# A planner that orders emission gets other prices: shared port, PSUM readers, table loads, products

## The chip, the cores and the metric

One core of one Trainium2 chip. The metric is the device time of one execution in microseconds, median of three runs. The core's engines run their own instruction queues in order: TensorE (PE; products, with PEld for the loading of weights), VectorE (DVE), ScalarE (ACT), GpSimd (POOL), and SyncE (SP), which issues most of the transfers.

## The reference

One inference step of a two-layer decoder trunk for 256 prompt tokens and 8 samples of 8 tokens, 320 tokens in all, width 2048, in fp32. Both groups share all weights.

```
layer 0:  h = modulate(x, c);  z = h @ ab_w_in
          GLA, 4 heads of 128 x 256, on q, k, v, r, g_lr out of z
          S5, 64 groups of 16 channels with 64 complex states, on u out of z
          y = y * sigmoid(y @ s5_w_glu + b);  x += gate * concat(o, y) @ ab_w_out
          h = modulate(x, c);  x += gate * (silu(h @ w1) * (h @ w3)) @ w2
layer 1:  h = modulate(x, c);  z = h @ ml_w_in
          mLSTM, 4 heads, matrix state 512 x 256 per head and sample
          x += gate * hh @ ml_w_out;  then a second FFN
final:    rmsnorm(x)
modulate(x, c): shift, scale, gate = silu(c) @ ada_w + ada_b, once for each of four sub-layers
```

The states of GLA, S5 and mLSTM are read, updated and written for every sample.

## The kernel before

**Products.** Every large product has the 320 tokens as its moving side. Weights come in units of 512 rows by 256 columns (`load_to`); `split_to` splits each into a rounded high part (ScalarE, `act.copy(hi, raw)`) and the rest (VectorE, `tensor_sub(lo, raw, hi)`), and `run_pair` does three products for each 128 x 128 block: high with high, low with high, high with low. Two rows of blocks and two columns make 12 products for each split of 128 x 512.

**Tasks beside the products.** After each block, `tick` may resume one or more of the Python generators that emit the recurrent layers: S5 (`s5_task`, `builder1`, `builder2`, `toep`, `gelu`, with the state scan largely on GpSimd), GLA (`gla_task` for four heads in turn, `gla_tail` for the state update of each head's eight samples), mLSTM (`ml_task`), and the modulation weights (`Ada`, whose `drip` does `run` steps every `gap` ticks; a step is four fp32 products of 32 rows, which stand in the trace as 8 records). A generator yields what it waits for: tiles, a number of ticks, or GO.

**The planner.** The order of all queues is fixed while the program is emitted, by a model of the engines. `Est` (line 130) keeps a time for each engine and, for every tile, when it is written and when it was last read. Each emitted operation goes through `note` (line 161), which adds a price to its engine's time. `tick` (line 383) resumes a task when

```
t[1] <= clock[0] and t[2] + SLACK <= est.t["PE"]
and max(est.t["DVE"], est.t["ACT"]) < est.t["PE"] + (AHEAD if t[3] >= 5 else AHS)
```

that is when its tiles are ready by the model's TensorE time and neither VectorE nor ScalarE is 2.5 us ahead. Tasks of lower rank number stand first in the list; S5's have ranks 1 to 4, GLA's 5. `mps` (line 279) picks, of three PSUM banks for small products, the one that the model sees free first. Where the main stream needs a result, `wait` (line 417) and `go` (line 404) emit a modulation step if one is ready (`spare`, line 508), else resume tasks, else emit a small warming product.

**Gates.** The output product of layer 0 runs first over S5's half of the rows, then over GLA's half, which needs the flags ("oh", h) of `conv` (line 1773), set after the last GLA head. A head's second part needs the flag of the previous head's tail, ("tail", h - 1). After mLSTM `z1_end` (line 2319) waits for the flag "nout" of the last head.

`toep` (line 1279) copies blocks out of one PSUM bank, `(act.copy if i % 2 else vec.tensor_copy)`, four by ScalarE, four by VectorE in turn. `gla_tail` does for each sample a mask on GpSimd (`km`), one product, and one VectorE addition.

Of the kernel before, what the change touches and what calls it, by code (L numbers as in the profile page):

```python
# [16 lines left out]
AF = mybir.ActivationFunctionType  # L17
# [5 lines left out]
T = 320  # L23
# [53 lines left out]
class Buf:  # L77
    def __init__(self, mem, off, n):
        self.mem, self.off, self.n = mem, off, n
# [50 lines left out]
class Est:  # L130
# [3 lines left out]
    def __init__(self):  # L134
        self.t = dict.fromkeys(("PE", "DVE", "ACT", "POOL", "SP", "DGE", "DMA"), 0.0)
        self.wr, self.rd, self.alias = {}, {}, {}
        self.end = 0.0

    def _at(self, tab, ap):
        t = ap.tensor  # L140
        name = self.alias.get(t.name, t.name)
        if ap.space == bass.MemoryType.DRAM:
            lo, hi = ap.offset, ap.offset + sum(st * (c - 1) for st, c in ap.ap)
            a = tab.setdefault(name, np.zeros(400 if len(name) < 8 else 1))
            o, n = (lo // 10240, hi // 10240 - lo // 10240 + 1) if len(a) > 1 else (0, 1)
        else:
            dims = list(ap.ap)
            row, parts = dims[0]
            a = tab.get(name)
            if a is None:  # L150
                a = tab[name] = np.zeros((4, row))
            q, o = ap.offset // row // 32, ap.offset % row
            quads = (ap.offset // row % 32 + parts + 31) // 32
            return np.lib.stride_tricks.as_strided(a[q:, o:], (quads, *(c for _, c in dims[1:])),
                                                   (8 * row, *(8 * st for st, _ in dims[1:])))
        return a[o:o + n]
# [4 lines left out]
    def note(self, eng, op, a, k):  # L161
        aps = [x for x in (*a, *k.values()) if isinstance(x, bass.AP)]
        out = k.get("out", aps[0])
        ins = [x for x in aps if x is not out and x is not k.get("accum_out")]
        n = int(np.prod(out.shape[1:]))
        t = self.t[eng]
        for x in ins:
            t = max(t, self.ready(x))
        if out.space != bass.MemoryType.DRAM:
            t = max(t, float(self._at(self.rd, out).max()))  # L170
            if eng != "PE" and op != "dma_start":
                t = max(t, self.ready(out))
        if op == "dma_start":
            if eng == "POOL":
                t = self.t[eng] = t + 1.2
            else:
                self.t[eng] = t + 0.06
                t = self.t["DGE"] = max(self.t["DGE"], t) + 0.45
            t = self.t["DMA"] = max(self.t["DMA"], t + 0.65) + 4e-3 * int(np.prod(out.shape)) / 360
            fin = t + 1.0  # L180
        else:
            if eng == "PE":
                if op == "transpose":
                    d = 0.107
                elif ins[0].shape[1] == 32:
                    d = 0.01 + 4.1e-4 * n
                elif ins[0].dtype == F32R:
                    d = n / 2400 + 0.003
                else:
                    d = max(1.67e-3 * n + 0.05, 0.2 + 5e-4 * n)  # L190
            elif eng == "ACT":
                d = 0.095 + 0.83e-3 * n
            elif eng == "POOL":
                d = 0.095 + n * (0.83e-3 if op == "memset" else 4e-3 if op == "tensor_scalar" else 2.27e-3)
            else:
                n = max(n, int(np.prod(ins[0].shape[1:]))) if op == "tensor_reduce" else n
                d = 0.065 + (6.26e-3 if op == "reciprocal" else 1.04e-3) * n
            t = self.t[eng] = t + d
            fin = t + 0.13
            self.end = max(self.end, fin)  # L200
        for x in ins:
            r = self._at(self.rd, x)
            np.maximum(r, fin, out=r)
        for x in (out, k.get("accum_out")):
            if x is not None:
                w = self._at(self.wr, x)
                np.maximum(w, fin, out=w)
# [26 lines left out]
def trunk(tc, a, o, coff, dbg=None, stop=None):  # L234
    nc = tc.nc
    est = Est()
# [3 lines left out]
    with (  # L240
# [163 lines left out]
        def go(gen):  # L404

            while True:
                est.end = 0.0
                try:
                    y = next(gen)
                except StopIteration as e:  # L410
                    return e.value
                p = est.t["PE"]
                idle(due(y)[1])
                if y is GO and est.t["PE"] == p:
                    idle(p + 0.3)
# [16 lines left out]
        class Ada:  # L432
# [75 lines left out]
            def spare(self):  # L508

                if self.s >= self.limit:  # L510
                    return False
                self.load()
                if est.ready(self.slot[self.s]) > est.t["PE"]:
                    return False
                return self.step()

# [5 lines left out]
            def drip(self):  # L522


                while self.s < 192:
                    n = min(self.run - self.s % self.run, self.last - self.s)
                    self.load()
                    if n <= 0:
                        if self.pend:
                            yield [ADAM["ev"].v(512)]  # L530
                            self.post()
                        yield self.gap
                    elif self.ld >= self.s + n and all(est.ready(self.slot[self.s + i]) <= est.t["PE"] for i in range(n)):
                        for _ in range(n):
                            self.step()
                        self.load()
                        yield self.gap
                    else:
                        yield 1
                self.post()  # L540
# [119 lines left out]
        n = 0  # L660
# [59 lines left out]
        def sums(sq):  # L720

            ps = yield from kept()
            for x, q in enumerate(sq):
                if x:
                    yield [q]
                for i, b in enumerate((0, P, 192)):
                    mm(ps[:, i:i + 1], q[:, b:b + P], ones[:, 0:1], x == 0 and i == 0, x == len(sq) - 1 and i == 2)
            yield 1
            return ps[:, 0:3]

        def rsqrt_tok(s, n):

            rs_n[0] ^= 1
            v, t, y = (rs_b.v(3, o=3 * i + 12 * rs_n[0]) for i in range(3))
            vec.tensor_scalar(v, s, 1.0 / n, EPS, MUL, ADD)
            drop(s)

            vec.tensor_scalar(y.bitcast(I32), v.bitcast(I32), 1, 0x3fffffff, ALU.logical_shift_right, ALU.bitwise_xor)
            vec.tensor_scalar(y, y, 0.957 * 2.0 ** 62.5, None, MUL)
            for _ in range(3):  # L740
                vec.scalar_tensor_tensor(t, y, -0.5, y, MUL, MUL)
                vec.tensor_mul(t, t, v)
                vec.scalar_tensor_tensor(y, t, 1.5, y, ADD, MUL)
            yield 1
            return y
# [81 lines left out]
        def resid(L, k, ps, sq):  # L827

            x, m = X[0], MOD[L]
            vec.scalar_tensor_tensor(x[:, k, 0:TP], ps[:, 0:TP], m[:, 32 + k, 0:1], x[:, k, 0:TP], MUL, ADD)  # L830
            t = gt_b.v(NB, 8, o=64 * (k % 2))
            vec.tensor_mul(t, ps[:, TP:T].rearrange("p (b t) -> p b t", b=NB),
                           m[:, 32 + k, 1:9, None].to_broadcast([P, NB, 8]))
            vec.tensor_add(x[:, k, TP:T], x[:, k, TP:T], gt_b.v(64, o=64 * (k % 2)))
            if sq:
                sq_chunk(k)
                if L == 3:
                    spawn(to_out(k), 0)
# [976 lines left out]
        for i in range(8):  # L1815
            add(Pair(a["ab_w_out"][0], 256 * i, 256, range(8, 16), act_opnd,
                     lambda j, ps, i=i: resid(0, 2 * i + j, ps, False)))
# [543 lines left out]
        n = len(first)  # L2361
# [57 lines left out]
        y = go(rsqrt_tok(go(sums([sq[:, i, :] for i in range(3)])), 2048))  # L2419
# [51 lines left out]
```

## Time and profile before

| | us |
|---|---|
| median of 3 runs | 3362.9 (3360.3 to 3363.32) |
| the profiled execution | 3362.54 |
| its span, first to last instruction | 3360.7 |
| TensorE busy | 3259.7 (97%) |
| VectorE busy | 1873.2 (56%) |
| ScalarE busy | 1328.4 (40%) |
| GpSimd busy | 332.8 (10%) |

In the trace all operations that go through the planner's wrapper carry line 220, so they are told apart by tile: `mm` are the large products, `ada` the modulation products, `misc` the small ones of the tasks, `hi` and `lo` the split weights, `S_slab` holds S5, `G_slab` and `GR_slab` hold GLA, `R_slab` mLSTM, `X_slab` the residual stream. An fp32 product stands as two records. Records of products overlap, so a product's spacing is read from a chain of many, not from its mean duration. "[7.01 <-DVE G_slab]" behind an instruction says that its engine stood idle for 7.01 us and what ended that.

### The profile page before, as it was taken

Reading aid. Unit: us, or ns where it says so; the run is one execution under the profiler, and the core shown is the slowest. Engines: PE = TensorE matmul, PEld = TensorE weight load, DVE = VectorE, ACT = ScalarE, POOL = GpSimd, SP = SyncE. Lnnn points to the kernel's source line nnn. Section 1 sums busy time; section 2 is a strip of 40 time slices with the busy share of each in tenths; the row PEclk is TensorE's granted clock in tenths of the full one; section 3 lists DMA queues with packets and bytes.
Section 4 is the critical chain, followed back from the end, with each engine's and each line's share of the span. In section 5 each row is a group of like instructions: output and inputs, shape, how many; then the busy total and the mean of one; then the engine's idle time right before and its main releaser. Section 6 shows DMA issues by size and latency. Waiting matters only on the chain.

```text
span 3360.7 us, 57787 instructions
## 1 busy us (share of the span) xinstructions
PE 3259.7 (97%) x22778; PEld 3036.6 (90%) x22778; DVE 1873.2 (56%) x3921; ACT 1328.4 (40%) x2509; POOL 332.8 (10%) x508
## 2 busy tenths in 40 slices
PE   7898899999999999999999999999999999999998
PEld 4687788998999989999998999999999999999997
DVE  3768667764444444444475665565644544545546
ACT  2364355343333333333434443344443343344343
POOL 0225411220000000000040000002200000000002
PEclk9999899999999999999999999999999999999999
DMA  9886688667767777776455664665444444444443
GB/s 304 295 266 235 205 307 301 237 235 255 258 235 273 240 255 257 236 274 201 150 165 144 194 187 140 187 188 201 145 151 151 151 151 151 150 149 150 149 150 101
DMA packets 597792, 686.66 MB, mean 204 GB/s; under 512 B 41096, under 2 KB 495056, under 8 KB 596944
## 3 DMA queue, kind: packets, MB, share of 16 engines
q1 hardware_dynamic: 594464, 680.26, 61.8%
q8 instruction: 179, 2.93, 0.3%
q10 hardware_dynamic: 3056, 2.70, 0.2%
q14 instruction: 93, 0.76, 0.1%
HBM read 643.19 MB, written 39.69 MB: 203 GB/s over the span
## 4 chain that ended last, share of the span: by engine, by line
PE 86%; DVE 5%; DMA 4%; ACT 2%; issue 1%; POOL 1%; SPq 1%; ACTq 0%; DVEq 0%; POOLq 0%
PE mm L220 73%; PE misc L220 8%; PE ada L220 4%; DVE lo L220 1%; DVE X_slab L220 1%; DVE S_slab L220 1%; POOL S_slab L220 1%; DMA fix_slab<-in_ab_ada_w_dram 1%; DVE xl L220 1%; SPq L220 1%; DMA UD<-S_slab 1%; DMA R_slab<-in_state_mlstm_C_dram 0%; DVE G_slab L220 0%; ACT hi L220 0%; DMA fix_slab<-in_ffn_ada_w_dram 0%
## 5 line engine op out<-in xcount | busy, mean ns | idle before, releaser
L220 DVE TENSOR_TENSOR lo<-fix_slab,hi 128x512 fp32r<-128x512 f32 (+1 forms) x1556 | 1089.1, 705 | 1155.2 <-ACT hi L220 1151.0
L220 PE MATMUL mm<-xh,hi 128*128 128x320 f32 x4704 | 1480.4, 315 | 10.7 <-DVE S_slab L220 7.6
L220 ACT CAST hi<-fix_slab 128x512 fp32r<-128x512 f32 (+1 forms) x1556 | 945.6, 612 | 1328.9 <-PE mm L220 1273.1
L220 PE MATMUL mm<-xh,lo 128*128 128x320 f32 x4704 | 1459.1, 310 | 1.4 <-DVE lo L220 1.4
L220 PE MATMUL mm<-xl,hi 128*128 128x320 f32 x4704 | 1459.7, 310 | 0.6 <-DVE xl L220 0.6
L220 PEld LDWEIGHTS mm<-xh,hi 128*128 128x128 f32 x4704 | 888.2, 189 | 57.5 <-issue 30.9
L220 PEld LDWEIGHTS mm<-xh,lo 128*128 128x128 f32 x4704 | 888.9, 189 | 2.8 <-DVE lo L220 2.3
L220 PEld LDWEIGHTS mm<-xl,hi 128*128 128x128 f32 x4704 | 888.1, 189 | 2.4 <-DVE xl L220 2.4
L220 PE MATMUL mm<-ffh,hi 128*128 128x320 f32 x1408 | 435.8, 310 | 0.0
L220 PE MATMUL mm<-ffh,lo 128*128 128x320 f32 x1408 | 434.3, 308 | 0.0
L220 PE MATMUL mm<-ffl,hi 128*128 128x320 f32 x1408 | 434.3, 308 | 0.0
L220 POOL TENSOR_TENSOR X_slab<-X_slab 128x320 f32<-128x320 f32 (+1 forms) x117 | 109.7, 938 | 2030.6 <-DVE X_slab L220 2015.3
L220 PEld LDWEIGHTS mm<-ffh,hi 128*128 128x128 f32 x1408 | 264.0, 188 | 6.7 <-issue 6.7
L220 PEld LDWEIGHTS mm<-ffh,lo 128*128 128x128 f32 x1408 | 264.0, 188 | 0.0
L220 PEld LDWEIGHTS mm<-ffl,hi 128*128 128x128 f32 x1408 | 264.0, 187 | 0.0
L220 PE MATMUL ada<-fix_slab 128*32 128x512 f32 x952 | 121.7, 616 | 6.4 <-DMA fix_slab<-in_ab_ada_w_dram 4.6
L220 POOL TENSOR_TENSOR S_slab<-S_slab 128x32 f32<-128x32 f32 (+3 forms) x226 | 114.1, 514 | 92.0 <-ACT S_slab L220 46.0
L220 ACT COPY fix_slab<-ada 128x512 f32<-128x512 f32 x48 | 28.1, 586 | 184.8 <-PE ada L220 184.8
L220 DVE SCALAR_TENSOR_TENSOR ffs<-ffs,mm 128x320 f32<-128x320 f32 x176 | 81.6, 488 | 22.8 <-ACT ffs L220 22.7
L220 DVE SCALAR_TENSOR_TENSOR X_slab<-mm,fix_slab,X_slab 128x256 f32<-128x256 f32 x176 | 84.6, 481 | 14.8 <-PE mm L220 14.8
L220 PEld LDWEIGHTS ada<-fix_slab 128*32 128x32 f32 x952 | 25.1, 111 | 56.7 <-issue 44.6
L220 DVE TENSOR_TENSOR S_slab<-S_slab 128x256 f32<-128x256 f32 (+3 forms) x167 | 70.6, 434 | 6.8 <-POOL S_slab L220 2.8
(153 smaller groups left out, 1923.2 us busy)
## 6 DMA issues: line engine op xcount, KB each, us to landing
fix_slab<-in_ffn_w_dram SPq DMA_DIRECT2D x524, 512.0 KB, 3.5
fix_slab<-in_ffn_ada_w_dram SPq DMA_DIRECT2D x65, 1024.0 KB, 8.7
fix_slab<-in_ml_w_in_dram SPq DMA_DIRECT2D x96, 512.0 KB, 4.7
fix_slab<-in_ab_ada_w_dram SPq DMA_DIRECT2D x35, 1024.0 KB, 7.7
fix_slab<-in_ab_w_in_dram SPq DMA_DIRECT2D x64, 512.0 KB, 7.0
adam<-in_ffn_ada_w_dram SPq DMA_DIRECT2D x31, 1024.0 KB, 8.2
adam<-in_ml_ada_w_dram SPq DMA_DIRECT2D x29, 1024.0 KB, 8.9
fix_slab<-in_ml_ada_w_dram SPq DMA_DIRECT2D x19, 1024.0 KB, 9.0
```

Source lines behind the costliest of these rows:

```text
L220: r = call(*a, **k)
```

## The change

`Est` alone is changed, and the two places that ask whether a modulation step's weights have landed. Operations, shapes and the tasks' code stay. Prices: a 320-column product in fp32r goes from n/2400 + 0.003 to n/2400 + 0.0135 us, the small fp32 products and the 32-row ones get new formulas, and changing between kinds of product costs 0.1 or 0.2. A result of TensorE is seen 0.2 instead of 0.13 us after its end. An operation that reads PSUM now starts only after the last reader of the bank on another engine. ScalarE pays 1.3 us when the function table changes (Ln, Sin, and all others that need one). The scan on VectorE costs twice as much per column. A GpSimd operation takes 15% longer when VectorE's time is ahead, and a VectorE operation with two or more inputs is lengthened by 0.9 of its overlap with the last 40 GpSimd operations. Weights of a modulation step must have been ready for 1 us.

```diff
@@ class Est, __init__
+        self.kind = self.table = None
+        self.bank = {}
+        self.pool = [(0.0, 0.0)] * 40
@@ note
         for x in ins:
             t = max(t, self.ready(x))
+            if x.space == bass.MemoryType.PSUM:
+
+                t = max([t] + [y for e, y in self.bank.get(self.alias.get(x.tensor.name, x.tensor.name), {}).items() if e != eng])
@@
                 if op == "transpose":
-                    d = 0.107
+                    kind, d = "other", 0.109
                 elif ins[0].shape[1] == 32:
-                    d = 0.01 + 4.1e-4 * n
+                    kind, d = "tiles", 4.23e-4 * n
                 elif ins[0].dtype == F32R:
-                    d = n / 2400 + 0.003
+                    kind, d = "stream" if n == T else "other", n / 2400 + 0.0135
                 else:
-                    d = max(1.67e-3 * n + 0.05, 0.2 + 5e-4 * n)
+                    kind, d = "other", max(1.667e-3 * n + 0.004, 0.222)
+
+                if kind != self.kind:
+                    d += 0.2 if "tiles" in (kind, self.kind) else 0.1
+                self.kind = kind
             elif eng == "ACT":
                 d = 0.095 + 0.83e-3 * n
+                fun = next((x for x in (*a, *k.values()) if isinstance(x, AF)), None)
+                if fun is not None and fun not in (AF.Identity, AF.Copy, AF.Square):
+                    table = fun if fun in (AF.Ln, AF.Sin) else "exp"
+                    if table != self.table:
+                        d += 1.3
+                    self.table = table
             elif eng == "POOL":
                 d = 0.095 + n * (0.83e-3 if op == "memset" else 4e-3 if op == "tensor_scalar" else 2.27e-3)
             else:
                 n = max(n, int(np.prod(ins[0].shape[1:]))) if op == "tensor_reduce" else n
-                d = 0.065 + (6.26e-3 if op == "reciprocal" else 1.04e-3) * n
+                d = 0.065 + (6.26e-3 if op == "reciprocal" else 2.1e-3 if op == "tensor_tensor_scan" else 1.04e-3) * n
+
+            if eng == "POOL" and op != "memset":
+                if self.t["DVE"] > t:
+                    d *= 1.15
+                self.pool = self.pool[1:] + [(t, t + d)]
+            elif eng == "DVE" and len(ins) > 1:
+                d += 0.9 * sum(max(0.0, min(t + d, y) - max(t, x)) for x, y in self.pool)
             t = self.t[eng] = t + d
-            fin = t + 0.13
+            fin = t + (0.2 if eng == "PE" else 0.13)
@@
         for x in ins:
+            if x.space == bass.MemoryType.PSUM:
+                self.bank.setdefault(self.alias.get(x.tensor.name, x.tensor.name), {})[eng] = fin
@@ spare
-                if est.ready(self.slot[self.s]) > est.t["PE"]:
+                if est.ready(self.slot[self.s]) + 1.0 > est.t["PE"]:
@@ drip
-                    elif self.ld >= self.s + n and all(est.ready(self.slot[self.s + i]) <= est.t["PE"] for i in range(n)):
+                    elif self.ld >= self.s + n and all(est.ready(self.slot[self.s + i]) + 1.0 <= est.t["PE"] for i in range(n)):
```

## Rows read from the trace of the kernel before

**Rows 1.** Windows: span; busy PE, PEld, DVE, ACT, POOL; clock; DMA share; GB/s
```profile
0.00:170.00 170.00, 137.23 (x849) 95.91 (x849) 93.56 (x271) 54.97 (x104) 24.44 (x44) 0.94 0.87 296
170.00:640.00 470.00, 436.74 (x3141) 376.25 (x3145) 335.25 (x893) 227.78 (x534) 139.51 (x275) 0.96 0.77 261
760.00:1680.00 920.00, 920.00 (x6452) 852.74 (x6452) 422.04 (x768) 332.82 (x569) 0.00 (x0) 1.00 0.70 240
1765.00:2275.00 510.00, 497.89 (x3697) 463.26 (x3697) 303.05 (x641) 202.81 (x395) 35.33 (x42) 0.99 0.58 174
2440.00:3270.00 830.00, 830.00 (x5661) 830.00 (x5660) 414.00 (x718) 325.36 (x554) 0.00 (x0) 1.00 0.48 150
```
**Rows 2.** Chain that ended last, dense stretch: start, us, what, how many
```profile
1600.48 142.13 PE mm L220 x969
```
**Rows 3.** Waits of PE in 170 to 640: us in total, times, longest
```profile
PE misc L220 <- ACT S_slab L220: 15.3, 6, 7.8
PE misc L220 <- DVE G_slab L220: 11.1, 6, 7.0
PE ada L220 <- DMA fix_slab<-in_ffn_ada_w_dram: 1.9, 2, 1.4
```
**Rows 4.** Timeline of PE, ACT: start, us, what, idle before and its releaser
```profile
335.44 1.97 PE L220 MATMUL misc<-S_slab 128*128 128x81 f32 x8 [7.01 <-DVE G_slab L220]
332.44 1.28 ACT L220 ACT_TABLE_LOAD   x1
393.81 0.55 PE L220 MATMUL misc<-GR_slab 96*128 96x256 f32 x1 [7.76 <-ACT S_slab L220]
392.80 0.91 ACT L220 COPY S_slab<-misc 32x128 f32<-32x128 f32 x4 [1.06 <-DVE S_slab L220]
```
**Rows 5.** Windows around the two stops, columns as in rows 1
```profile
328.00:346.00 18.00, 10.99 (x61) 10.20 (x61) 12.47 (x34) 8.39 (x23) 12.26 (x31) 0.53 0.63 219
390.00:404.00 14.00, 9.89 (x46) 7.94 (x50) 7.66 (x27) 7.13 (x22) 2.50 (x4) 0.52 0.44 124
```
**Rows 6.** Windows of the large products' tile alone: PE, PEld, DVE, ACT
```profile
170.00:640.00 470.00, 277.12 (x1716) 255.99 (x1716) 21.24 (x57) 12.47 (x28) 0.96 0.77 261
1765.00:2275.00 510.00, 367.48 (x2291) 341.19 (x2291) 0.00 (x0) 21.15 (x49) 0.99 0.58 174
```
**Rows 7.** Timeline of VectorE around 385: additions beside GpSimd, alone, and a split
```profile
380.48 5.93 DVE L220 TENSOR_TENSOR S_slab<-S_slab 128x256 f32<-128x256 f32 x8
387.53 1.80 DVE L220 TENSOR_TENSOR S_slab<-S_slab 128x256 f32<-128x256 f32 x4
389.25 0.69 DVE L220 TENSOR_TENSOR lo<-fix_slab,hi 128x512 fp32r<-128x512 f32 x1
```
**Rows 8.** GpSimd's groups in 252 to 420: count, busy us, mean ns, idle
```profile
L220 POOL TENSOR_TENSOR S_slab<-S_slab 128x32 f32<-128x32 f32 x128 | 41.3, 322 | 9.7
L220 POOL TENSOR_TENSOR S_slab<-S_slab 128x256 f32<-128x256 f32 x42 | 33.0, 805 | 42.1 <-ACT S_slab L220 41.0
```
**Rows 9.** Groups of ScalarE in 170 to 640: the table loads
```profile
L220 ACT ACT_TABLE_LOAD x9 | 11.5, 1283 | 0.1
```
**Rows 10.** Timeline of PE before the output product's second half
```profile
638.95 1.92 PE L220 MATMUL ada<-fix_slab 128*32 128x512 f32 x16
```
**Rows 11.** Timeline of PE at the end of mLSTM
```profile
2273.21 1.92 PE L220 MATMUL ada<-fix_slab 128*32 128x512 f32 x16
```
**Rows 12.** Waits of PE in 1765 to 2275, for the state blocks
```profile
PE misc L220 <- DMA R_slab<-in_state_mlstm_C_dram: 2.5, 5, 1.7
```
**Rows 13.** Timeline of PE: first and last state product of tails 0, 1
```profile
280.04 0.36 PE L220 MATMUL misc<-GR_slab 96*128 96x256 f32 x1
433.13 0.39 PE L220 MATMUL misc<-GR_slab 96*128 96x256 f32 x1
461.60 0.28 PE L220 MATMUL misc<-GR_slab 96*128 96x256 f32 x1
479.50 0.28 PE L220 MATMUL misc<-GR_slab 96*128 96x256 f32 x1
```

## The prediction, made before the change was run

> **What bounds the kernel now.** I read the busy time by stage first, because the change alters no product, no transfer and no formula; it can only alter the order in which instructions stand in the queues, and that matters only where an order is free. In the two dense stages (760 to 1680 and 2440 to 3270, together 1750 of the span's 3360.7 us) TensorE shows no idle time at all [rows 1]: products follow each other at 142.13 us for 969, 0.1467 us each [rows 2]. No task runs there except the loading of modulation products every 70 ticks, so these 1750 us stand. The first 170 us move 296 GB/s with the 16 DMA engines busy 0.87 of the time; they wait for weights, and no price of an engine changes that. What is left to an order are 170 to 640 (S5 and GLA beside the products of layer 0), 1765 to 2275 (mLSTM), and small stretches around the norms. TensorE is idle 33.3 us of the 470 in the first and 12.1 of the 510 in the second.
>
> Then I read who is waited for. In 170 to 640 two names carry it: products of S5 and GLA wait 15.3 us in 6 waits for ScalarE and 11.1 in 6 for VectorE [rows 3]. The two longest are in the timeline [rows 4]. At 328.2 TensorE stops 7.01 us for a product of S5 whose PSUM bank GLA had not yet read out: a table load of 1.28 us and a scan lie ahead of that read. At 386 it stops 7.76 us for a GLA tail product whose operand ScalarE copies only after the block copies of `toep`, where VectorE and ScalarE read one bank in turns (ScalarE waits 1.06 us for its second turn). Around each stop the granted clock is near one half: 0.53 over 328 to 346 and 0.52 over 390 to 404 [rows 5], that is the lower level, 1.2 GHz, for most of it, after TensorE had stood or done little. With 10.99 and 9.89 us of busy time there, running at 0.53 and 0.52 costs 5.2 and 4.7 us. The ceiling of the first stage is thus 33.3 + 9.9 = 43.2 us.
>
> **The change part by part.** It emits no new operation; the planner `Est` only gets other prices, and tasks are resumed at other places of the stream.
> The *product price* goes from 320/2400 + 0.003 = 0.1363 to 0.1468 us against the row's 0.1467. With 1716 products in the first free stage and 2291 in the second [rows 6] the planner's TensorE clock gains 18.0 and 24.1 us. So far a task whose data were due in L us came back after L/0.1363 products, 7.7% later in real time than needed; that cushion goes. Small fp32 products get cheaper (81 columns 0.2405 to 0.222) and each change of kind 0.1 or 0.2 us dearer; these two nearly cancel, I take nothing for them.
> The *shared port*: a VectorE addition of 128x256 takes 1.80/4 = 0.45 us alone and 5.93/8 = 0.74 beside GpSimd [rows 7]. The planner had 0.331 for both and now adds 0.9 of the overlap. GpSimd's own operations were priced 0.168 (128x32) and 0.676 (128x256); the rows of 252 to 420 have 0.322 and 0.805 [rows 8]. The new factor of at most 1.15 gives 0.193 and 0.777.
> *One reader per bank*, *table loads* (9 of 1.283 us in the stage [rows 9], priced 1.3, zero until now) and the *scan* (0.40 to 0.74) are the causes of the two long stops. I take both stops away, 14.8 us, and their slow clock, 9.9; of the other waits for ScalarE and VectorE (15.3 + 11.1 - 14.8 = 11.6) half, 5.8. That is 30 us by which TensorE gets through its products sooner; the ends are 0 and 43.
> *Ready plus 1.0* on modulation steps: it can save the 1.9 us of such waits in the stage [rows 3], and puts each step 1 us later; cover is that the steps of this stage are needed only at the norm behind the gate below, and if that cover were gone a step would cost the wait for its weights. I take nothing. The transfers that tasks issue on SP move with them; between 170 and 640 the DMA engines have 0.77 of their time taken [rows 1], so this too is nothing, with the range bearing it.
>
> **Where the 30 us go** is the question that decides. The output product of layer 0 needs the GLA heads. At 638.95 TensorE does two modulation steps as a filler (16 records, 1.92 us) [rows 10]: the planner had nothing else, because the flag of GLA was still missing. So products and GLA chain end together now. If products come 30 us sooner, TensorE stands before that gate from about 609 on, and GLA ends when it ends. Its chain is not sped up by a missing TensorE stall as such: in the 7.01 us stop VectorE and ScalarE were working for GLA. It is sped up by what is no longer beside it: each 12 products (1.76 us) cost VectorE one split of 0.69 us [rows 7], 39% of it, and VectorE is busy 335 of 470 us. For 30 us without them I take one third off the chain, 10 us (ends 0 and 30). In the other 20 us modulation steps fill in: two loaded ones and about two more, 0.96 us each by the gate's row, 4 us that later stages need not do. A slow clock after standing costs some back, 3 us. Sum: 10 + 4 - 3 = 11 us.
> The second stage ends at the same kind of gate: 16 filler records at 2273.21 [rows 11]. GpSimd hardly works there (35 of 510 us), its stops are short and partly for DMA. Without the cushion tasks come back sooner; I take 1 us of gain, the ends being -12 (all idle time) and +16 (all 32 state blocks waited for, at the 2.5/5 = 0.5 us that five of them cost now [rows 12]). The profiled execution took 3362.54, 1.84 over its span, and the median is 3362.9: no correction is needed. 3362.5 - 12 = **3350 us**.
>
> **The rivals.**
> *All of it is kept* (3328). The chain of GLA shortens as much as the products do, because ScalarE and VectorE, in order, no longer hold each other up at the bank and at GpSimd. For it: tail 1's eight steps took 17.9 us (461.60 to 479.50) where tail 0's took 153 (280.04 to 433.13) [rows 13], so there is room. Against: S5 runs beside tail 0 and keeps its VectorE work. 30 us plus 5 in the other stage: 3328, between 3310 and 3338.
> *The GLA tail starves longer* (3384). Tail 0 is a task of low rank; it comes back only while VectorE in the plan is less than 2.5 us ahead of TensorE. Dearer VectorE work beside GpSimd makes that rarer. One more turn missed is one step of tail 0, 153/7 = 21.9 us, and head 1 waits for the tail, head 2 for head 1, the gate for head 3. It decides from the point where the chain ends later than 638.95: 3362.5 + 22 = 3384.
> *GpSimd stays underpriced* and nothing moves (3362). Between 252 and 420 its rows are 128 x 0.322 + 42 x 0.805 = 75 us; the old prices give 49.9, the new ones at most 57.4. Some 17 us stay unseen, operands that GpSimd makes are still expected too early, and stops of the present size stand at other places. The Trainium skill, "SBUF — State Buffer", section "Who interferes with whom", says that the shared pair is an exclusive lock and that whichever engine starts second is blocked outright, so that either may be the loser; it speaks against charging VectorE 0.9 and GpSimd only 0.15 of its time. The rows of GpSimd agree with that as far as they go.
>
> **How the numbers follow.** Forecast case 0.36 (3338 to 3358), all kept 0.22, starving tail 0.25 (3368 to 3400), nothing moves 0.17 (3356 to 3369). A measurement of this kernel tells apart about 0.2%, 6.7 us: faster is below 3356.2, slower above 3369.6. Faster: 0.22 + 0.32 = 0.54; slower 0.26; same 0.20. The range goes from 3318 to 3386: below lies a third of the all-kept case (0.07), above a part of the starving one (0.10). The forecast's own range is 3338 to 3358.
>
> **What would show it.** Right: the waits of 7.0 and 7.8 us are gone, the granted clock between 320 and 420 is near 1, the first S5 output and tail 0 come no later, and before the output product of layer 0 more than two modulation steps stand in a row with warming products among them, VectorE's splits missing there. Wrong towards fast: the gate is reached with no filler at all. Wrong towards slow: tail 0's last product comes after 433, and the filler is long. If GpSimd is the matter, stops of 5 us and more remain between 250 and 420. The dense stages must keep 0.1467 us per product; if they don't, the whole reading is wrong.

## The result and the profile after

The changed kernel takes **3388.9 us** (3383.2 to 3391.8 in four runs); the kernel before took 3363.1 beside it. The ratio is 1.0079, 95% interval 1.0066 to 1.0093: slower, and above the range of 3318 to 3386. The span grew from 3360.7 to 3389.0 us.

To see where the 28.3 us lie, I cut each trace at the first of the small warming products that stand at each norm. Between them lie the same large products in both kernels: 2544 up to the end of layer 0's mixing, 6336 in each FFN, 3120 in mLSTM.

| | layer 0 mixing | first FFN | mLSTM | second FFN |
|---|---|---|---|---|
| before | 697.5 | 1047.1 | 646.3 | 954.7 |
| after | 700.2 | 1047.3 | 679.6 | 946.8 |
| difference | +2.7 | +0.2 | **+33.3** | -7.9 |

So the loss is in mLSTM, where the prediction saw 1 us of gain, and the gain of layer 0, which it saw at 11, is not there. The windows by stage of the kernel after (they answer to [rows 1]; the last is moved by 30 us because its stage begins later):

```profile
170.00:640.00 470.00, 437.93 (x3127) 377.35 (x3126) 326.59 (x872) 222.18 (x525) 133.89 (x275) 0.96 0.78 257
1765.00:2275.00 510.00, 475.67 (x3453) 438.96 (x3452) 284.31 (x599) 190.96 (x377) 31.70 (x40) 0.97 0.55 163
2470.00:3300.00 830.00, 830.00 (x5661) 830.00 (x5661) 414.57 (x719) 325.03 (x554) 0.00 (x0) 1.00 0.48 150
```

In mLSTM TensorE is idle 34.3 of 510 us (12.1 before), at a mean clock of 0.97 instead of 0.99. The dense stage is as it was; in the chain that ended last it reads, with the end of layer 0 above it (start, us, what, how many):

```profile
635.32 62.93 PE mm L245 x429
2453.26 869.86 PE mm L245 x5931
```

869.86/5931 is 0.1467 us, the product of [rows 2].

**mLSTM.** PE's waits of 1765 to 2275, after, answer to [rows 12] (us in total, times, longest):

```profile
PE misc L245 <- DMA R_slab<-in_state_mlstm_C_dram: 24.6, 21, 2.3
PE misc L245 <- ACT R_slab L245: 2.5, 5, 0.5
PE misc L245 <- DMA R_slab<-in_state_mlstm_n_dram: 2.4, 1, 2.4
```

The waits for the state blocks went from 2.5 us in 5 to 24.6 in 21, that is 22.1 of the 33.3. The trace's records of the granted clock put 34.1 us of the stage at the lower level, 1.2 GHz, against 13.7 before; by an estimate, work done in 20.4 us at half speed would have taken 10.2 less (TensorE stood idle in 0.8 of the 34.1 us). Together that is 32.3. Where the clock falls is less clear than the waits: 17.1 of the 34.1 us lie ahead of the first wait for a block, where before has its 13.7; of the five stretches of 3.4 us behind it one begins at a wait for a block (at 2000.4, 2.3 us) and three just behind a wait of 0.5 us for ScalarE, which the kernel before has too, without a fall.

How a wait for a block arises stands in the timeline of PE and SP after (start, us, engine, what, idle before it and its releaser; SPq is SP issuing a transfer), first PE's:

```profile
1882.51 1.06 PE L245 MATMUL misc<-fix_slab,R_slab 128*128 128x128 f32 x8 [1.50 <-DMA R_slab<-in_state_mlstm_C_dram]
1887.90 1.06 PE L245 MATMUL misc<-fix_slab,R_slab 128*128 128x128 f32 x8 [0.32 <-DMA R_slab<-in_state_mlstm_C_dram]
1895.69 1.06 PE L245 MATMUL misc<-fix_slab,R_slab 128*128 128x128 f32 x8 [1.84 <-DMA R_slab<-in_state_mlstm_C_dram]
```

and SP's:

```profile
1883.77 0.37 SPq L245 DMA_DIRECT2D R_slab<-in_state_mlstm_C_dram  x1
1884.74 0.50 SPq L245 DMA_DIRECT2D out_dram<-R_slab  x1
1891.18 0.37 SPq L245 DMA_DIRECT2D R_slab<-in_state_mlstm_C_dram  x1
1891.65 0.45 SPq L245 DMA_DIRECT2D out_dram<-R_slab  x1
1897.07 0.37 SPq L245 DMA_DIRECT2D R_slab<-in_state_mlstm_C_dram  x1
```

Three buffers `CR` hold the blocks. While block g is worked on, the task issues the store of block g - 1 and then, into the same buffer, the load of block g + 2, which waits until that store has landed. The next store stands behind this load in SP's queue. So the queue passes one block for each landing of a store: 1884.74 to 1891.18 and 1891.65 to 1897.07 are landings, the 0.5 to 1.0 between are issues. The block loaded at 1891.18 is the one that TensorE waits for at 1895.69. Over the stage the median from store to load is 5.4 us, and the 26 distances between loads within a head are 6.22 us on average. Before, the same chain ran at 7.65 us; SP there:

```profile
1882.70 0.37 SPq L220 DMA_DIRECT2D R_slab<-in_state_mlstm_C_dram  x1
1883.66 0.51 SPq L220 DMA_DIRECT2D out_dram<-R_slab  x1
1890.10 0.37 SPq L220 DMA_DIRECT2D R_slab<-in_state_mlstm_C_dram  x1
```

There too SP stood before a landing for 6.4 of 7.4 us, but TensorE had work for as long. In the emitted order 26.6 large products stood on average between two state blocks; the new prices put 15.9 there, 10.7 x 0.1467 = 1.6 us less work. But on TensorE the ends of two blocks within a head came only 0.7 us closer, from 6.5 to 5.8 us (28 distances): its wait rose from 0.1 to 0.9 us a block (24.6/28), and that is about the rest. The planner knows the chain: `note` lets a load begin only when the store out of its buffer has landed, and holds SP's queue until then. But it prices each of these transfers, from issue to landing, at 0.45 + 0.65 + 1.46 + 1.0 = 3.6 us. The trace's DMA issues after say 4.4 and 5.6 (what, count, KB, median us to landing):

```profile
R_slab<-in_state_mlstm_C_dram SPq DMA_DIRECT2D x32, 512.0 KB, 4.4
out_dram<-R_slab SPq DMA_DIRECT2D x32, 512.0 KB, 5.6
```

and before:

```profile
R_slab<-in_state_mlstm_C_dram SPq DMA_DIRECT2D x32, 512.0 KB, 4.0
out_dram<-R_slab SPq DMA_DIRECT2D x32, 512.0 KB, 6.3
```

The stage still ends at its gate with 16 filler records, 36 us later than in [rows 11] (timeline of PE):

```profile
2309.43 1.92 PE L245 MATMUL ada<-fix_slab 128*32 128x512 f32 x16
```

**Layer 0.** The two stops of [rows 4] are gone. PE's waits of 170 to 640 after, against [rows 3]:

```profile
PE misc L245 <- DMA S_slab<-UD: 7.8, 2, 7.3
PE misc L245 <- ACT S_slab L245: 4.7, 3, 2.5
PE misc L245 <- DVE G_slab L245: 4.4, 6, 1.4
```

For S5 and GLA on ScalarE and VectorE 9.1 us are left of 26.4; a new wait of 7.3 us for S5's own load stands between 170 and 240. The windows of [rows 5], and the 100 us around them, after:

```profile
328.00:346.00 18.00, 18.00 (x129) 15.97 (x130) 16.40 (x41) 6.63 (x18) 5.13 (x6) 0.91 0.89 290
390.00:404.00 14.00, 13.13 (x107) 11.84 (x109) 6.25 (x22) 5.48 (x19) 10.60 (x30) 1.00 0.69 236
320.00:420.00 100.00, 94.99 (x711) 80.31 (x709) 75.10 (x191) 46.49 (x122) 42.50 (x97) 0.97 0.76 244
```

and before:

```profile
320.00:420.00 100.00, 78.11 (x558) 65.50 (x561) 69.96 (x193) 41.72 (x118) 43.51 (x99) 0.83 0.63 199
```

In these 100 us TensorE gets 17 us more busy time, at 0.97 instead of 0.83 of its clock. Large product 1500 starts at 438.3 instead of 489.8, in part because S5's small products now stand behind it. All of it is given back at a gate, yet another one than the prediction named. The window of the large products' tile alone, after:

```profile
486.00:511.00 25.00, 0.00 (x0) 0.00 (x0) 0.98 (x2) 0.88 (x2) 1.00 0.94 308
```

For 25 us not one large product runs, at full clock, because the output product over S5's rows comes next and S5 is not ready. The timeline of those us, after:

```profile
481.33 3.33 PE L245 MATMUL misc<-S_slab 128*128 128x81 f32 x24
493.26 2.42 PE L245 MATMUL misc<-fix_slab 128*128 128x128 f32 x18
503.16 0.34 SPq L245 DMA_DIRECT2D S_slab<-YD  x1
506.71 1.83 PE L245 MATMUL misc<-fix_slab 128*128 128x128 f32 x14
```

S5's last products stand at 481 to 485, where before its last were at 441 (behind 1578 large products of the emitted order, before behind 1308). What S5 gives is loaded back at 503.2, and until 511 warming products (`misc<-fix_slab`), modulation steps and GLA's small products fill the queue. The last state product of tail 0 comes at 444.6, against 433.1 in [rows 13]; GLA's gate at 639 [rows 10] is passed with no filler at all, in the chain of 429 products quoted above.

### The profile page after: what moved, and what is told of

It reads as the page before. It is cut to its first block, busy times and chain, and to the rows that moved or that the text cites. A ratio compares the mean times of both kernels' runs of the same rounds, so it can differ in the third digit from the quotient of the medians.

```text
span 3389.0 us, 57907 instructions
## 1 busy us (share of the span) xinstructions
PE 3281.9 (97%) x22836; PEld 3058.1 (90%) x22836; DVE 1875.5 (55%) x3921; ACT 1327.1 (39%) x2509; POOL 324.6 (10%) x506
## 4 chain that ended last, share of the span: by engine, by line
PE 80%; DMA 7%; DVE 7%; ACT 2%; issue 2%; POOL 1%; SPq 0%; ACTq 0%; DVEq 0%; POOLq 0%
PE mm L245 69%; PE misc L245 7%; PE ada L245 4%; DMA R_slab<-in_state_mlstm_C_dram 2%; DVE lo L245 2%; DVE G_slab L245 1%; DVE S_slab L245 1%; DMA YD<-S_slab 1%; POOL S_slab L245 1%; DMA out_dram<-R_slab 1%; DVE xl L245 1%; ACT hi L245 1%; DVE fix_slab L245 1%; SPq L245 0%; DMA fix_slab<-in_ffn_ada_w_dram 0%
## 5 line engine op out<-in xcount | busy, mean ns | idle before, releaser
L245 PE MATMUL misc<-fix_slab 128*128 128x128 f32 (+1 forms) x488 | 80.6, 292 | 4.6 <-DVE X_slab L245 1.9
L245 PEld LDWEIGHTS misc<-fix_slab 128*128 128x128 f32 x488 | 65.2, 176 | 19.6 <-issue 6.6
```

Source lines behind the costliest of these rows:

```text
L245: r = call(*a, **k)
```

## The experiments

"Before" in a description is the kernel before with the named prices of the change; all other prices stay old. `mixing`, `mLSTM`, `FFN 2` are stage lengths of the profiled execution, cut as above; `blocks` is PE's wait for state blocks there (us, times); `half` is the time of mLSTM at the lower clock. Seven profiles whose emitted order up to the end of mixing is that of before (before itself, the three with late prices) or that of after (after and two more) put that stage at 692.7 to 697.5 and 700.2 to 706.7, so 5 to 6.5 us in one profile say nothing, the +2.7 of after among them. The means of the two orders, 694.5 (four profiles) and 703.6 (three), are 9 us apart: the changed order does lose in layer 0.

| run | us | ratio (95%) | mixing | mLSTM | FFN 2 | blocks | half |
|---|---|---|---|---|---|---|---|
| before | 3363.1 | | 697.5 | 646.3 | 954.7 | 2.5, 5 | 13.7 |
| after | 3388.9 | 1.0079 (1.0066-1.0093) | 700.2 | 679.6 | 946.8 | 24.6, 21 | 34.1 |
| pe_alone | 3417.5 | 1.0163 (1.0140-1.0186) | 712.2 | 682.5 | 951.1 | 23.8, 17 | 34.1 |
| no_pe | 3365.7 | 1.0007 (0.9997-1.0018) | 713.8 | 645.4 | 947.1 | 5.9, 9 | 17.1 |
| switch_alone | 3395.8 | 1.0101 (1.0079-1.0122) | 706.7 | 672.0 | 955.2 | 12.2, 10 | 34.1 |
| stream_alone | 3392.2 | 1.0091 (1.0068-1.0114) | 709.8 | 661.7 | 951.1 | 9.5, 12 | 27.3 |
| half_blocks | 3364.2 | 1.0007 (0.9993-1.0021) | 706.7 | 651.9 | 947.9 | 4.1, 5 | 17.1 |
| state_price | 3366.0 | 1.0008 (0.9995-1.0020) | 703.8 | 648.1 | 948.2 | 6.1, 8 | 13.7 |
| nudge | 3359.1 | 0.9992 (0.9981-1.0002) | 689.8 | 648.2 | 953.1 | 3.7, 7 | 20.5 |
| late_alone | 3343.7 | 0.9942 (0.9921-0.9962) | 694.2 | 636.9 | 945.3 | 2.7, 3 | 6.8 |
| late_port | 3347.1 | 0.9959 (0.9945-0.9972) | 693.7 | 648.4 | 945.2 | 3.1, 5 | 23.9 |
| late_mlp | 3341.6 | 0.9929 (0.9905-0.9953) | 692.7 | 633.2 | 945.6 | none | 6.8 |
| pe_state | 3388.4 | 1.0073 (1.0048-1.0097) | 713.9 | 654.0 | 952.3 | 6.3, 5 | 20.5 |
| port_alone | 3366.5 | 1.0003 (0.9992-1.0014) | 710.2 | 648.0 | 945.2 | 2.5, 2 | 23.9 |

### Which half of the change: pe_alone and no_pe

pe_alone is before with TensorE's prices, the switch charges and the 0.2; no_pe is after without them.

```diff
@@ pe_alone, against after
-            if x.space == bass.MemoryType.PSUM:
...
-                    if table != self.table:
-                        d += 1.3
-            if eng == "POOL" and op != "memset":
...
-            elif eng == "DVE" and len(ins) > 1:
...
-                if est.ready(self.slot[self.s]) + 1.0 > est.t["PE"]:
+                if est.ready(self.slot[self.s]) > est.t["PE"]:
@@ no_pe, against after
-                if kind != self.kind:
-                    d += 0.2 if "tiles" in (kind, self.kind) else 0.1
-                    kind, d = "stream" if n == T else "other", n / 2400 + 0.0135
+                    d = n / 2400 + 0.003
...
-            fin = t + (0.2 if eng == "PE" else 0.13)
+            fin = t + 0.13
```

> The kernel before with the TensorE prices alone (product times, kind changes, 0.2 us to a result); port, banks, tables, scan and the 1.0 us stay as before. Theory A (TensorE's prices bring the mLSTM tasks back after 15.9 products per state block instead of 26.6, too soon for the state transfers): the mLSTM stage loses about what it loses in the changed kernel, 33 us between the norm before it and the norm behind it, with 20 or more waits for state transfers. The last GLA state product is emitted after 1872 large products instead of 2133, so no filler before the output product of layer 0 and a gain of 10 to 25 us up to the first FFN. Sum 3370 to 3390 us. Rival B (the transfers are late because the first stages moved, whatever the order in mLSTM): mLSTM loses less than 10 us here, sum 3340 to 3360.

> The changed kernel without the TensorE prices (product times, kind changes and the 0.2 us as before); port, banks, tables, scan and the 1.0 us are in. Theory A: mLSTM keeps 26.7 products per state block and loses under 3 us against before; layer 0 has the last S5 product after 1584 large products instead of 1308, so TensorE waits before the S5 gate product and the first stage is 5 to 30 us longer than before; sum 3368 to 3393 us. Rival B: mLSTM still loses over 20 us, sum over 3385. Rival C (port, banks and tables are what gains and TensorE's prices lose everything): below 3350.

TensorE's prices alone give the whole loss of mLSTM (682.5), and without them it is gone (645.4). In layer 0 both halves lose, where a gain of 10 to 25 was expected of pe_alone, and so its time, 3417.5, lies above the expected 3370 to 3390. Its TensorE does not stop at a gate of S5, but keeps stops (window of PE, 320 to 420, pe_alone: busy 82.1, clock 0.88):

```profile
320.00:420.00 100.00, 82.11 (x589) 64.78 (x593) 71.42 (x193) 46.87 (x126) 52.90 (x111) 0.88 0.65 212
```

Which of them make its loss was not followed further. no_pe stands at the gate of S5 for 86 us with 3 large products (window of their tile, no_pe):

```profile
442.00:528.00 86.00, 0.71 (x3) 0.45 (x3) 0.97 (x2) 0.44 (x1) 1.00 0.82 257
```

### Which of TensorE's prices: switch_alone and stream_alone

```diff
@@ switch_alone, against before: old prices of products, but
+                if kind != self.kind:
+                    d += 0.2 if "tiles" in (kind, self.kind) else 0.1
+                self.kind = kind
@@ stream_alone, against before
-                    d = n / 2400 + 0.003
+                    d = n / 2400 + 0.0135
```

> The kernel before with nothing but the charges of 0.1 and 0.2 us for a change between kinds of product. It has 17.5 products per state block. Theory A1 (the kind charges are the larger part of what shortens the blocks): mLSTM loses 20 to 33 us. Theory A2 (it is the price of the large product): mLSTM loses under 8 us. GLA's last state product after 1824 products: the first stage gains 5 to 25 us.

> The kernel before with nothing but the new price of the fp32r products (0.1468 instead of 0.1363 us). It has 23.1 products per state block. Theory A1: mLSTM loses 3 to 10 us. Theory A2: 20 to 33 us. GLA's last state product after 2022 instead of 2133 products: the first stage gains 0 to 10 us.

The switch charges, which the prediction took at nothing, put 17.5 products between two blocks and cost mLSTM 25.7 us; the price of the large product puts 23.1 there and costs 15.4. The fewer products, the longer the waits for blocks, and the time at the lower clock goes with them in these runs. Neither gains in layer 0 (+9 and +12), where 5 to 25 and 0 to 10 were expected, and the product price costs mLSTM more than the 3 to 10 us that theory A1 gave it.

### Is it the round trip of the state blocks: half_blocks and state_price

half_blocks keeps TensorE's order of after and halves the bytes of the transfers: it leaves out the second half of each state block, in the loads from the fourth block on and in every store. state_price keeps the bytes and makes the planner think a block is there 4.0 us later, which puts 25.0 products between blocks.

```diff
@@ half_blocks, against after
+                    y = slice(0, 4 if g < 3 else 2)
+                    nc.sync.dma_start(out=full["out"][:, y], in_=full["in_"][:, y])
+                    est.note("SP", "dma_start", (), full)
@@ the store, likewise
+                    nc.sync.dma_start(out=full["out"][:, 0:2], in_=full["in_"][:, 0:2])
@@ state_price, against after, behind the load
+                    est._at(est.wr, CR[g % 3].v(4, 256))[...] += 4.0
```

> The changed kernel in the very same order of TensorE, but from the fourth mLSTM state block on only half of each block is read from and written to memory (the planner still prices whole ones); the other half of those state outputs is left out. Theory D (the 15.9 products per block are too few for the state transfers, which come late): waits for state blocks fall from 24.6 us to under 6, and mLSTM, 679.6 us between the norms in the changed kernel and 646.3 in the one before, falls to 643 to 660; sum 3355 to 3370 us. Rival E (short blocks leave the hops between TensorE, ScalarE and VectorE uncovered, the transfers only come last): mLSTM stays over 670 and the waits turn to ScalarE and VectorE; sum over 3380.

> The changed kernel with one more price: each mLSTM state block counts as landed 4 us later in the plan. That gives 25.0 products per state block instead of 15.9 (26.6 in the kernel before); all up to mLSTM is in the same order as in the changed kernel. Theory D: mLSTM falls from 679.6 to 643 to 657 us, sum 3355 to 3368 us. Rival E2 (what lengthens mLSTM is the order at other places, gates or heads, that TensorE's prices also moved): mLSTM over 670, sum over 3380.

PE's wait in half_blocks and its DMA issues:

```profile
PE misc L245 <- DMA R_slab<-in_state_mlstm_C_dram: 4.1, 5, 1.4
R_slab<-in_state_mlstm_C_dram SPq DMA_DIRECT2D x29, 256.0 KB, 3.8
out_dram<-R_slab SPq DMA_DIRECT2D x32, 256.0 KB, 4.4
```

With half the bytes a store lands in 4.4 instead of 5.6 us, the loads follow each other at 5.07 instead of 6.22, the blocks on TensorE at 5.0 instead of 5.8, and 27.7 of the 33.3 us are gone with not one instruction of TensorE moved. More products between the blocks, at full bytes (loads every 7.10 us), take 31.5 off. The transfers of the state blocks against TensorE's work between two blocks are the cause. That it is the ring, in which a load waits for a store and holds the queue, is read from the timelines; no run gave it a fourth buffer or put the stores on another queue.

### Are the two losses separate: pe_state

pe_alone with state_price's line.

> pe_alone (TensorE's new prices alone, 1.0163) with 4.0 us more in the plan for each mLSTM state block. The part of layer 0 stands in the order of pe_alone. If the two losses of pe_alone are independent (theory S), mLSTM returns to 646 to 650 and layer 0 keeps its loss of 10 to 15: 3376 to 3386. Rival: what layer 0 lost was scatter of the runs, or comes from the same blocks: 3362 to 3370.

mLSTM comes back to 654.0, short of the expected 646 to 650, mixing stays at 713.9, the time at 1.0073. The loss of TensorE's prices in layer 0 is real and has nothing to do with the blocks.

### How much does an order vary: nudge

```diff
@@ against before
-                    d = n / 2400 + 0.003
+                    d = n / 2400 + 0.0035
```

> The kernel before with the price of the fp32r product raised by 0.0005 us alone (0.1368 instead of 0.1363), a step that says nothing on the hardware. Theory F (the first stage's end, 697.5 us before and 700 to 714 in the variants, scatters with any change of order, because two gates meet there): it moves by 3 us or more, either way; sum between 3350 and 3380 us. Rival G (the first stage answers smoothly to prices): it stays within 2 us, sum 3360 to 3366.

0.0005 us on the product price changes the emitted order from large product 669 on. Its one profile has mixing 7.7 us shorter than that of before, but only 4.7 below the mean of the four profiles of before's order, which lie 5 us apart; the time is 0.9992, an interval that still holds 1. So no effect clear of the scatter is shown. The change's own 0.0105 went the other way, and beyond it (stream_alone, 709.8).

### The other prices, in layer 1 alone: late_alone, late_port and port_alone

late_alone turns the port, the bank reader, the tables, the scan and the 1.0 us on at the first FFN and keeps TensorE's old prices; late_port does that with the port alone; port_alone has it from the start.

```diff
@@ late_alone, against before: the port's price
+            if self.on and eng == "POOL" and op != "memset":
...
+            elif self.on and eng == "DVE" and len(ins) > 1:
...
@@ where the program is put together, ahead of layer 0's FFN
+        prog.append(lambda: setattr(est, "on", True))
         prog.append(lambda: norm_h(1))
```

> The kernel before up to the first FFN (the old prices rule the first stage), then port, banks, tables, scan and the 1.0 us of the change, but never its TensorE prices. Theory H (these edits are worth something where no gate takes it back: 3.2 us in the first FFN, 0.9 in mLSTM and 7.6 in the second FFN, as without the TensorE prices): first stage 697.5 as before, sum 3348 to 3355 us. Rival I (those gains come from what the first stage leaves behind): sum 3358 to 3368 us.

> Before's prices up to the first FFN, and from there on the shared-port price alone; the bank reader, table loads, scan and the 1.0 us stay out. late_alone, with all five from that place, gave 0.9942. Theory P: the port price is the one that gains in layer 1, because it alone parts the last norm's small products into threes (before they stand in sixes that wait for VectorE 12 times) and shifts the mLSTM tasks: 3340 to 3350, last norm region as in late_alone (the last 336 products of the second FFN 53 us instead of 60), mLSTM 635 to 646. Rival Q: the gain needs the bank reader or the table price as well, or was scatter between orders: 3355 to 3364.

> Before with the shared-port price alone, from the start. Layer 1 has the order of late_port; in layer 0 the last S5 product stands behind 1584 large products instead of 1308. Theory G: the port price loses in layer 0 what it gains in layer 1, because S5 ends at a gate: layer 0's mixing ends 8 to 18 us later, layer 1 gains 10 to 19: 3355 to 3366. Rival: the long gate of no_pe came from the bank reader or the tables, and the port price alone is as good as late_port: 3340 to 3350.

late_alone beats both kernels, by more than expected, and the port price brings most of it: with it alone FFN 2 is 9.5 us shorter. Of these 3.4 lie in its first 200 large products and 6.2 at its very end, where the last norm's small products stand between the last 336 large ones. The groups of PE there, before (from 2440 on):

```profile
L220 PE MATMUL misc<-fix_slab,X_slab 128*128 128x128 f32 (+1 forms) x66 | 10.3, 273 | 3.9 <-DVE X_slab L220 3.9
```

and late_port (3200 to 3330):

```profile
L231 PE MATMUL misc<-fix_slab,X_slab 128*128 128x128 f32 x36 | 5.9, 273 | 0.0
```

Before, they came six at a time and waited for VectorE in 11 places; with the port priced they come in threes and don't wait. 3.9 of the 6.2 us by which these 336 products take less are those waits; the rest was not placed. In the kernel after, four of the six groups still come as sixes and don't wait either, so the threes alone are not shown to be the reason. port_alone has the same FFN 2 (945.2) and loses it in mixing (+12.7), where S5's last products are pushed behind 1584 large ones and the gate is reached with 43 us to fill (window of the large products' tile, port_alone):

```profile
474.00:517.00 43.00, 0.00 (x0) 0.00 (x0) 0.98 (x2) 0.87 (x2) 1.00 0.78 246
```

late_port's mLSTM (648.4) missed the expected 635 to 646. That late_alone has the shorter one (636.9) comes in its trace, for 8.2 of the 11.5 us, from the first 400 products of the stage, 83.6 us against 91.8, the one place where the order of TensorE differs from late_port's; the two times have overlapping intervals, so this stays likely and no more.

### A better version: late_mlp

late_alone with 2.0 us on each state block in the plan.

> late_alone, and each mLSTM state block priced 2.0 us dearer in the plan. By count the products between two blocks go from 12 to 36 unevenly (two of 12 and 15 in a row) to 21 to 36, with one short gap per sample group. Theory D (the round trip of a state block sets what a short gap costs): the waits for state blocks fall from 2.7 to about 1 us and mLSTM gains 1 to 5 us: 3338 to 3344. Rival: the gaps were long enough already and the shift takes other work with it: 3344 to 3352.

3341.6, 0.9929 (0.9905 to 0.9953), the fastest of all: no wait for a state block is left. Its advance over late_alone is inside both intervals.

## Why the prediction was wrong, point by point

- **What bounds the kernel**: right. The dense stages kept 0.1467 us a product, "these 1750 us stand", and what moved lies in the two free stages and at norms. The "small stretches around the norms" were named and then stand in the sum with nothing: the second FFN's -7.9 us lie there, 1.6 in its first 200 large products and 6.3 at the last norm, where small products stand among the large ones. The row for the latter was the short waits for `X_slab`, which the prediction didn't read.
- **The stops of layer 0**: right. Both are gone, with their slow clock: 17 us more work in 320 to 420. A wait of 7.3 us came up elsewhere.
- **The gate that keeps the gain**: right in kind, wrong in place. The 30 us were to end at GLA's gate at 639, with 11 kept. They ended at S5's, 128 us earlier, for S5 itself was put off: 270 products later in the order. The port price does this by itself (S5's last products behind 1584 large ones in port_alone), TensorE's prices don't (behind 1269 in pe_alone). The prediction's own sign, that tail 0 should "come no later", failed (444.6 for 433.1), and S5's last products came at 485 for 441. By the stages, mixing measured +2.7 for -11 (+9 by the means of the two orders): 14 of the 40 us by which the sum is off (+28.3 for -12).
- **The starving tail**: the rival had the mechanism (dearer VectorE work brings a task back later) and put it on the wrong task. Tail 0 lost 11.5 us, not 21.9, and the gate behind it was met; S5 was the one that starved.
- **mLSTM, the step that failed most**: 34 of the 40 us (the second FFN's -7.9 counts against both). The text says that "tasks come back sooner", which they did, and took 1 us of gain with a bound of +16, from 32 blocks at 0.5 us each. The bound priced the waits of the old order. In the new one 21 blocks wait 1.17 us each, and TensorE's clock is at its lower level for longer, an estimated 10 us more. The chain could have been read from the trace of before: SP stood before the landing of a state store for 6.4 us of the 7.4 from load to load in the lines above, so a task that comes back sooner finds no transfer that could be sooner by as much. The prediction looked only at PE's waits, and these were small because TensorE happened to have as much work.
- **"These two nearly cancel, I take nothing for them"**: wrong. The switch charges alone move mLSTM by 25.7 us, more than the product price (15.4) that the prediction worked out. Alone they bring the products between two blocks from 26.6 to 17.5, the product price to 23.1: each state block passes through several changes of kind, so these charges are the larger part of what the plan's TensorE clock gains there.
- **GpSimd stays underpriced**: no. The sign for this rival, stops of 5 us and more between 250 and 420, isn't there, although the operations of [rows 8] still take 305 and 754 ns (322 and 805 before). The Trainium skill, "SBUF — State Buffer", section "Who interferes with whom", has either engine as the possible loser. In layer 1 the price that charges VectorE most of it gained 0.4% (late_port); no run varied GpSimd's share.

## What to carry to other kernels

Truer prices for some operations don't make a truer planner: a price that brings a task back sooner spends a cushion on which another delay lived that is priced too low, here the landing of each store (3.6 us in the plan, 5.6 in the trace), for which the queue of the next load waits. Before such a change, look beside PE's waits at what the issuing queue stands for, since a ring whose queue waits all the time has no room even where nobody waits for it yet. And a gain ahead of a gate is worth only what the gate's own chain gains; look which gate comes first.

## What the runs showed of the hardware

- Transfers of 512 KB landed 4.4 us (load) and 5.6 us (store) after their issue in the kernel after, 4.0 and 6.3 in the kernel before; those of 256 KB 3.8 and 4.4 (half_blocks). The Trainium skill, "DMA: Bandwidth & Descriptors", section "Anatomy of one DMA — SWDGE (gpsimd) path", gives, for another way of issuing, a fixed 2.0 us and the bytes at 436 GB/s, by which an estimate would be 3.2 and 2.6. Set beside after and half_blocks, the loads' difference of 0.6 agrees with it, with 1.2 us more in both; the stores' difference of 1.2 doesn't, and they take 1.8 and 2.4 more.
- TensorE's clock stood at 1.2 GHz for 34.1 us of an mLSTM stage with 21 waits of about 1 us for blocks, and for 17.1 and 13.7 where these were mostly gone (half_blocks, state_price). By the estimate above the longer time at the lower level cost 10.2 us beside the 22.1 of the waits. The waits for blocks are not all of it: late_port has 23.9 us at the lower level with five waits, 3.1 us in all.
